# Tree attention on Trainium2: one quad of heads stored by two engines, by heads and by uneven partitions

## The chip, the cores and the metric

The kernel runs on one core of one Trainium2 chip. The metric is device microseconds of one launch. The core has five engines with instruction streams of their own: PE (TensorE, matrix products and transposes), DVE (VectorE), ACT (ScalarE), POOL (GpSimd) and SP (SyncE, which here only issues DMAs). Data moves between HBM and the on-chip memory through 16 DMA engines. GpSimd, SyncE and ScalarE issue transfers; each has its own queue (q0, q1 and q10 in the profile) on every one of the 16.

## The reference

Attention with 8 batches of 12 heads, 512 positions of 64 numbers, in float32. Position i may look only at itself and its ancestors in the binary tree in which the parent of i is (i - 1) // 2.

```python
for i in range(seq):
    mask[i, i] = 1
    parent = i
    while parent > 0:
        parent = (parent - 1) // 2
        mask[i, parent] = 1
scores = np.einsum('bhqd,bhkd->bhqk', Q, K) * scale + (1 - mask) * (-1e9)
weights = np.exp(scores - np.max(scores, axis=-1, keepdims=True))
weights = weights / (np.sum(weights, axis=-1, keepdims=True) + 1e-10)
return np.einsum('bhqk,bhkd->bhqd', weights, V).astype(np.float32)
```

The output is 96 heads x 512 x 64 float32, 12.58 MB; the first store is issued at 61.9 us.

## The kernel before, in words

The 96 heads are worked in 48 **pairs** (NP = 48, index i) and stored in 24 **quads** of four heads (NQ = 24, index q); quad q is done when the second of pairs 2q and 2q + 1 is. Position 4p + t of a head lies on partition p in slot t, so in HBM a partition's part of one head is one contiguous run of 4 x 64 float32, 1 KB.

For each pair, TensorE transposes K and Q (lines 401 and 433 in the steady part), adds mask codes to the scores by matrix products (458 and 491) and adds the products of K and Q (466 and 501). ScalarE takes the exponentials (476 and 507), TensorE multiplies by V with a column of ones (`values`, 551), and `norm` on VectorE divides by the sum (581, 582) into the output tile `of` of the quad, 128 partitions x 4 heads x 256. There are NOUT = 22 such tiles. The steady iteration is "SVK" or "SVQ": scores of pair i, values and norm of pair i - 1, transposes ahead.

All loads of K, Q and V but the first are issued by GpSimd, in an order written out in `pool_program` (lines 608 to 639); `pool(i)` emits as many of them after iteration i as `ready` allows. That list also has GpSimd's copies of V and the stores: `store` (589) writes one quad, 128 partitions x 4 heads x 1 KB = 512 KB. Eight of the stores stand among the loads, 13 at the list's end. The order in the list is the order of GpSimd's queue.

Quad 19, which holds pairs 38 and 39, is left out of that list. `store_apart` (600) gives it to SyncE after iteration 41, in two DMAs of all four heads: partitions 0 to 59 (240 KB) and 60 to 127 (272 KB). Quads 20 and 21 are GpSimd's again, its last two stores. The last two quads are stored by pairs (lines 768 and 769): SyncE issues two heads (256 KB) for each of pairs 44, 45 and 46 after iterations 45, 46 and 47. The last pair's heads go out singly: SyncE writes one (771), ScalarE the other (772), 128 KB each.

GpSimd's DMAs use eight completion semaphores in turn, so each of its DMAs waits until the eighth one before it has landed. SyncE's transfers share one queue per DMA engine and are worked there in the order of issue.

Of the kernel before, what the change touches and what calls it, by code (L numbers as in the profile page):

```python
# [119 lines left out]
def kernel(  # L120
# [7 lines left out]
    nc = tc.nc  # L128
    B, H, S, D = Q.shape
    P = nc.NUM_PARTITIONS  # L130
# [3 lines left out]
    NQ = NH // 4  # L134
# [17 lines left out]
    Or = out.rearrange("b h (p t) d -> p (b h) (t d)", t=4)  # L152
# [76 lines left out]
    qTs, kTs, kqs, obs, ets, ofs = {}, {}, {}, {}, {}, {}  # L229
# [365 lines left out]
        )  # L595


    APART, APART_AT, APART_ROWS = 19, 41, 60

    def store_apart():  # L600

        for p0, p1 in ((0, APART_ROWS), (APART_ROWS, P)):
            nc.sync.dma_start(
                out=Or[p0:p1, 4 * APART:4 * APART + 4, :],
                in_=ofs[APART][p0:p1, :, :, :].rearrange("p h t d -> p h (t d)"),
            )

    def pool_program():

        ops = [  # L610
            (load_k, 2, 2), (load_q, 2, 2), (load_v, 0, 4), (load_v, 4, 4),
            (load_k, 4, 2), (load_k, 6, 2), (load_q, 4, 2), (load_k, 8, 4),
            (load_q, 6, 2), (load_q, 8, 4), (load_v, 8, 8), (load_k, 12, 4),
            (load_q, 12, 4), (load_k, 16, 4), (load_rows, 1, "upper"),
            (load_q, 16, 4), (load_rows, 1, "even"), (load_k, 20, 4), (load_rows, 1, "odd"),
            (load_q, 20, 4), (load_k, 24, 8), (load_q, 24, 4), (load_rows, 2, "upper"),
            (load_q, 28, 4), (load_k, 32, 4), (load_rows, 2, "even", "odd"),
            (load_q, 32, 8), (load_k, 36, 4), (load_rows, 3, "upper"),
            (load_k, 40, 8), (load_rows, 3, "even", "odd"),
            (load_q, 40, 8), (spread_top, 2, 0, 16), (spread_top, 3, 0, 4), (load_q, 48, 4),  # L620
            (spread_top, 3, 4, 8), (load_k, 48, 8), (load_q, 52, 4), (spread_top, 3, 8, 12),
            (load_rows, 4, "upper"), (spread_top, 3, 12, 16),
        ]
        loaded, stored = 72, 0
        for h in range(56, NH, KB):
            top = [(spread_top, h // VB + 0)] if h % VB == 8 and 4 <= h // VB + 0 < NH // VB else []
            ops += [(load_k, h, KB)] + top + [(load_q, h, KB)]
            while loaded < min(h + 32, NH):
                names = ("even", "odd") if loaded % VB else ("upper",)
                ops.append((load_rows, loaded // VB) + names)  # L630
                loaded += KB
            if top:
                o = h // VB
                ops.append((spread_pool, (o, "X", 0, 16), (o, "Z1", 8, 16)))
            while 4 * stored + 4 + BEHIND <= h + KB:
                ops.append((store, nc.gpsimd, stored))
                stored += 1
        ops += [(store, nc.gpsimd, q) for q in range(stored, NQ - 2) if q != APART]
        return ops

    def ready(op, i):
# [62 lines left out]
    def spread_by(copy, table, steady, i):  # L704
# [5 lines left out]
        for args in todo:  # L710
            spread(copy, *args)

    program = pool_program()

    def pool(i):
# [21 lines left out]
    for i in range(NP + 1):  # L737
        steps = FIRST[i] if i < len(FIRST) else "SVK" if i % 2 else "SVQ"
        for step in steps:
# [11 lines left out]
            if step == "W":  # L751
                nc.scalar.copy(
                    out=codes[64:64 + CODE_ROWS, 1280:1536], in_=codes[0:CODE_ROWS, 1280:1536]
# [12 lines left out]
        if i == APART_AT:  # L766
            store_apart()
# [35 lines left out]
```

## Time and profile before

| what | value |
|---|---|
| median of 3 runs | 135.13 us (134.98 to 135.68) |
| the profiled execution's own time | 136.0 us |
| its span, first to last instruction | 132.8 us |
| around the span (136.0 - 132.8) | 3.2 us |
| busy: PE, DVE, ACT, POOL | 86%, 77%, 77%, 53% of the span |
| bytes read and written in HBM | 37.94 MB, 12.58 MB |
| mean granted TensorE clock | 0.979 |

A busy share is an average over the span. The page's second part shows each engine in 40 slices, a digit for tenths of busy time; for DMA it is the mean of the 16 DMA engines, so 8 may mean that all pause a little or that three have nothing to do. For every DMA the trace has a line with the time from issue to landing. It also holds the record of each packet (start, duration, size, queue) and of every update of a DMA's semaphore: each DMA engine that carries a part adds its share when that part has landed. All times in this document are us from the start of the span.

### The profile page before, as it was taken

Reading aid. Unit: us, or ns where it says so; the run is one execution under the profiler, and the core shown is the slowest. Engines: PE = TensorE matmul, PEld = TensorE weight load, DVE = VectorE, ACT = ScalarE, POOL = GpSimd, SP = SyncE. Lnnn points to the kernel's source line nnn. Section 1 sums busy time; section 2 is a strip of 40 time slices with the busy share of each in tenths; the row PEclk is TensorE's granted clock in tenths of the full one; section 3 lists DMA queues with packets and bytes.
Section 4 is the critical chain, followed back from the end, with each engine's and each line's share of the span. In section 5 each row is a group of like instructions: output and inputs, shape, how many; then the busy total and the mean of one; then the engine's idle time right before and its main releaser. Section 6 shows DMA issues by size and latency. Waiting matters only on the chain.

```text
span 132.8 us, 5554 instructions
## 1 busy us (share of the span) xinstructions
PE 114.1 (86%) x2414; PEld 79.2 (60%) x2417; DVE 101.8 (77%) x253; ACT 102.7 (77%) x169; POOL 70.6 (53%) x110
## 2 busy tenths in 40 slices
PE   6787969999899899779999999979898997989830
PEld 2344745766675677456775677657576675756520
DVE  3449769889999999945899998858796976757260
ACT  4379578988899999937899989958886987696900
POOL 6999525364343908999323369863976524512000
PEclk9999999999999999986999999999999999999996
DMA  3999999999999999999999999999999999999982
GB/s 98 245 189 192 199 198 200 201 202 206 200 202 203 202 204 198 209 205 201 205 204 196 316 254 204 292 274 242 330 214 335 233 297 402 401 399 397 373 322 70
DMA packets 32380, 32.25 MB, mean 243 GB/s; under 512 B 1341, under 2 KB 29629, under 8 KB 32357
## 3 DMA queue, kind: packets, MB, share of 16 engines
q0 software_dynamic: 29984, 29.63, 114.3%
q1 hardware_dynamic: 1813, 1.83, 4.0%
q10 hardware_dynamic: 560, 0.46, 1.1%
q8 instruction: 18, 0.29, 0.8%
q14 instruction: 5, 0.04, 0.1%
HBM read 37.94 MB, written 12.58 MB: 381 GB/s over the span
## 4 chain that ended last, share of the span: by engine, by line
DMA 38%; PE 29%; POOL 14%; issue 7%; ACT 5%; DVE 3%; POOLq 0%; ACTq 0%; DVEq 0%
DMA vst<-in_V_dram 20%; PE ob L551 10%; DMA qst<-in_Q_dram 10%; DMA kst<-in_K_dram 9%; PE s L458 4%; POOL vt L336 4%; PE s L491 3%; PE s L501 3%; PE qtp L433 3%; PE ktp L401 3%; PE s L466 3%; POOL kst L239 3%; POOL qst L239 3%; ACT e L507 3%; POOL vst L239 2%
## 5 line engine op out<-in xcount | busy, mean ns | idle before, releaser
L476 ACT ACTIVATE e<-s 128x1024 bf16<-128x1024 f32 x40 | 40.8, 1021 | 14.6 <-PE s L466 14.1
L551 PE MATMUL ob<-vt,e 128*128 128x65 bf16 (+1 forms) x940 | 37.9, 198 | 4.2 <-issue 2.0
L551 PEld LDWEIGHTS <-e 128*128 128x128 bf16 (+1 forms) x960 | 30.7, 103 | 12.5 <-issue 2.5
L507 ACT ACTIVATE e<-s 128x384 bf16<-128x384 f32 x80 | 34.6, 488 | 0.0
L582 DVE TENSOR_TENSOR of<-ob,rec 128x512 f32<-128x512 f32 x47 | 32.5, 691 | 1.6
L590 POOL DMA_DIRECT2D out_dram<-of x21 | 15.9, 761 | 16.7 <-DVE of L582 5.0
L336 DVE COPY vt<-vst 32x1024 bf16<-32x1024 bf16 (+6 forms) x46 | 19.7, 427 | 2.6 <-DMA vst<-in_V_dram 1.8
L581 DVE RECIPROCAL rec<-ob 128x8 f32<-128x8 f32 x47 | 9.7, 205 | 15.0 <-PE ob L551 14.7
L458 PE MATMUL s<-codes 40*128 40x512 bf16 x96 | 19.6, 398 | 0.8 <-ACT e L472 0.4
L466 PE MATMUL s<-kq 64*128 64x512 bf16 x96 | 18.8, 382 | 0.0
L336 POOL COPY vt<-vst 32x128 int32<-32x128 int32 (+2 forms) x32 | 15.7, 492 | 5.7 <-DMA vst<-in_V_dram 3.4
L280 POOL DMA_DIRECT2D vst<-in_V_dram x15 | 10.9, 728 | 10.6 <-DMA vst<-in_V_dram 5.4
L336 ACT COPY vt<-vst 32x512 int32<-32x512 int32 (+3 forms) x29 | 15.9, 550 | 0.7 <-DMA vst<-in_V_dram 0.2
L501 PEld LDWEIGHTS <-kq 64*128 64x128 bf16 x320 | 12.5, 95 | 5.4 <-issue 1.2
L501 PE MATMUL s<-kq 64*128 64x160 bf16 (+1 forms) x320 | 15.2, 211 | 0.5 <-issue 0.5
L441 DVE COPY kq<-qtp 128x1024 bf16<-128x1024 bf16 x20 | 13.6, 681 | 1.7 <-PE qtp L433 1.7
L491 PE MATMUL s<-codes 40*128 40x384 bf16 x80 | 13.9, 339 | 0.8
L433 PE MATMUL qtp<-ptile,qst 128*64 128x128 bf16 x320 | 12.5, 219 | 2.3 <-DMA qst<-in_Q_dram 1.7
L251 POOL DMA_DIRECT2D kst<-in_K_dram x12 | 9.0, 753 | 10.0 <-DMA kst<-in_K_dram 3.4
L401 PE MATMUL ktp<-ptile,kst 128*64 128x128 bf16 x320 | 13.0, 224 | 1.2 <-issue 0.8
L251 POOL DMA_DIRECT2D qst<-in_Q_dram x13 | 9.5, 733 | 6.9 <-PE qtp L433 2.1
L491 PEld LDWEIGHTS <-codes 40*128 40x128 bf16 x80 | 6.3, 95 | 10.8 <-issue 4.2
(42 smaller groups left out, 121.6 us busy)
## 6 DMA issues: line engine op xcount, KB each, us to landing
out_dram<-of POOLq DMA_DIRECT2D x21, 512.0 KB, 12.7
kst<-in_K_dram POOLq DMA_DIRECT2D x8, 512.0 KB, 13.5
qst<-in_Q_dram POOLq DMA_DIRECT2D x7, 512.0 KB, 13.9
vst<-in_V_dram POOLq DMA_DIRECT2D x12, 256.0 KB, 13.0
vst<-in_V_dram POOLq DMA_DIRECT2D x6, 512.0 KB, 13.0
qst<-in_Q_dram POOLq DMA_DIRECT2D x8, 256.0 KB, 11.0
kst<-in_K_dram POOLq DMA_DIRECT2D x6, 256.0 KB, 12.0
out_dram<-of SPq DMA_DIRECT2D x3, 256.0 KB, 5.4
```

The lines of the kernel that those rows point to most:

```text
L251: return nc.gpsimd.dma_start(out=kept[b][:, h0 % KB:h0 % KB + n, :, :].rearrange("p (g x) t d -> p g (x t d)", x=2), in_=wide[:, h0 // 2:( ...
L336: return copy(out=dst, in_=src)
L401: nc.tensor.transpose(out=columns(kp[64 * a:64 * a + 64, :], mixed, (256, 2), (leaves - mixed, 2), (1, 32)), in_=st[:, 2 * i % KB // 2 + a ...
L433: nc.tensor.transpose(out=halves[64 * a:64 * a + 64, :, c:c + 64], in_=st[:, 2 * i % KB // 2 + a, 4 * u + t, :], identity=ptile[:, 0:128],)
L458: nc.tensor.matmul(out=sp[:, a, :], lhsT=(k1code if i < WIDE else k1wide)[64 * a:64 * a + CODE_ROWS, :], rhs=(q1code[64 * a:64 * a + CODE_ ...
L466: nc.tensor.matmul(out=sp[:, a, :], lhsT=keys(i, a, TOP), rhs=qTs[i][64 * a:64 * a + 64, :, :].rearrange("p t c -> p (t c)"), start=False, ...
L476: ) if i < WIDE else nc.scalar.activation(
L491: nc.tensor.matmul(out=flat[:, a, :, :].rearrange("p u (t c) -> p u t c", t=4)[:, :, :, 16:64], lhsT=k2wide[64 * a:64 * a + CODE_ROWS, :], ...
L501: nc.tensor.matmul(out=flat[:, a, :, lo:hi], lhsT=keys(i, a, WTILE2[t]), rhs=qT[64 * a:64 * a + 64, :, lo:hi], start=False, stop=t == 1, s ...
L507: nc.scalar.activation(out=e2s[i % NE][:, a, :, 32:128].rearrange("p t (r u) -> p t r u", u=2), in_=flat[:, a, :, :].rearrange("p u (t r) ...
L551: nc.tensor.matmul(out=ob[lo:hi, a, 65 * t:65 * t + 65], lhsT=e[:, a, PLACE[t], lo:hi], rhs=vt[vtile[tile_v][0]][:, head(i, a) % VB, vtile ...
L582: nc.vector.tensor_tensor(out=ofs[q][:, head(i, a) % 4:head(i, a + n - 1) % 4 + 1:head(i, 1) - head(i, 0), :, :], in0=o4[:, a:a + n, :, 0: ...
```

## The change

Quad 19 is split by heads. SyncE stores heads 0 and 1 of it, as before in 60 and 68 partitions, after iteration 41. GpSimd stores heads 2 and 3 in 12 and 116 partitions, between quads 18 and 20 in its list. No bytes are added or taken away. `ready` treats the new entry as it does a store of quad 19.

```diff
-    APART, APART_AT, APART_ROWS = 19, 41, 60
+    APART, APART_AT, APART_ROWS, FEW_ROWS = 19, 41, 60, 12
+
+    def store_rows(eng, q, h0, *bounds):
+
+        for p0, p1 in zip(bounds, bounds[1:]):
+            eng.dma_start(
+                out=Or[p0:p1, 4 * q + h0:4 * q + h0 + 2, :],
+                in_=ofs[q][p0:p1, h0:h0 + 2, :, :].rearrange("p h t d -> p h (t d)"),
+            )
 
     def store_apart():
 
-        for p0, p1 in ((0, APART_ROWS), (APART_ROWS, P)):
-            nc.sync.dma_start(
-                out=Or[p0:p1, 4 * APART:4 * APART + 4, :],
-                in_=ofs[APART][p0:p1, :, :, :].rearrange("p h t d -> p h (t d)"),
-            )
+        store_rows(nc.sync, APART, 0, 0, APART_ROWS, P)
...
-        ops += [(store, nc.gpsimd, q) for q in range(stored, NQ - 2) if q != APART]
+        for q in range(stored, NQ - 2):
+            if q == APART:
+                ops.append((store_rows, nc.gpsimd, q, 2, 0, FEW_ROWS, P))
+            else:
+                ops.append((store, nc.gpsimd, q))
         return ops
```

## Prediction

> **What bounds the kernel now.** I read the slices first, then the stretches of the end, the chain of waits, the issue times of the stores, and last the single landings.
>
> In the page's slices the transfer engines stand at 9 from the second slice to the last but two:
>
> ```profile
> DMA  3999999999999999999999999999999999999982
> ```
>
> The table by stretches of the end (PE, PEld, DVE, ACT and POOL busy, clock, DMA share, GB/s) shows who is full there:
>
> ```profile
> 118.00:122.00 4.00, 3.28 (x78) 2.41 (x75) 2.40 (x7) 2.89 (x6) 0.75 (x1) 1.00 1.04 405
> 122.00:126.00 4.00, 3.42 (x66) 2.13 (x62) 1.53 (x3) 3.82 (x8) 0.00 (x0) 1.00 0.98 376
> 126.00:130.00 4.00, 1.17 (x22) 0.86 (x22) 2.02 (x6) 0.21 (x1) 0.00 (x0) 1.00 0.88 316
> 130.00:132.80 2.80, 0.00 (x0) 0.00 (x0) 0.00 (x0) 0.00 (x0) 0.00 (x0) 0.61 0.09 31
> ```
>
> The DMA share is about 1 until 126 us and 0.88 to 130: some of the 16 DMA engines have run out of work, others have not. The end of the chain of waits and the last stores on ACT's and SyncE's timelines:
>
> ```profile
> 127.46 0.42 DVE of L582
> 127.89 0.10 DVE rec L581
> 127.99 0.02 issue
> 128.01 0.43 DVE of L582
> ```
>
> ```profile
> 128.47 0.36 ACTq L590 DMA_DIRECT2D out_dram<-of  x1
> ```
>
> ```profile
> 110.32 0.93 SPq L603 DMA_DIRECT2D out_dram<-of  x2
> 122.66 5.61 SPq L590 DMA_DIRECT2D out_dram<-of  x4
> ```
>
> Compute ends at 128.44, the last store is issued at 128.47, and the span ends at 132.8. So two things bound the end: the compute chain, which the change does not touch, and how long the last store takes. From the DMA part:
>
> ```profile
> out_dram<-of SPq DMA_DIRECT2D x1, 272.0 KB
> ...
> out_dram<-of SPq DMA_DIRECT2D x1, 240.0 KB, 8.5
> ...
> out_dram<-of ACTq DMA_DIRECT2D x1, 128.0 KB, 3.1
> ```
>
> The 3.1 us of the last store is the number to take apart. The trace records a semaphore update for each DMA engine's share. ACT's store landed on ten engines between 130.03 and 130.18, on the other six at 130.48, 130.67, 130.88, 130.97, 131.26 and 131.56. Without a backlog it would be over at 130.18; the backlog of six engines costs 131.56 - 130.18 = **1.38 us**, all that a better balance can win.
>
> Who are the six? The 240 KB store (60 partitions) has 15 such landings, the 272 KB one (68 partitions) only **four**: 126.52, 126.70, 128.59, 128.89. It puts 17 rows, 68 packets of 1 KB, on each of four engines. Behind it SyncE's queue holds 16 + 16 + 16 + 8 packets per engine, and ACT's 8: 64 in all. Packets of 1 KB follow each other in 42.3 ns (packet records after 130 us), so 64 take 2.71 us; 128.59 and 128.89 plus 2.7 are 131.3 and 131.6, the two last landings. Two of the four engines with the 68 rows thus end the kernel; the other two are in time. The remaining four late engines carry only ordinary work; the worst lands at 130.97.
>
> How early are the others? SyncE's store of pair 44 (issued at 122.66) landed on three engines by 125.59, on seven between 127.37 and 128.09, on the six late ones from 128.48 to 129.55. A late engine's landing plus 2.01 is its last landing, so lateness begins at about 130.1 - 2.0 = 128.1: three engines have over 2 us of slack, seven have 0 to 0.7.
>
> **The change, part by part.** Bytes are the same (512 KB); only their placing changes.
>
> 1. *SyncE's two stores halve.* Fifteen engines have 4 rows of 2 KB where they had 4 of 4 KB: 8 packets fewer, 8 x 42.3 ns = -0.34 us. Four engines have 17 rows of 2 KB: 34 packets fewer, -1.44 us. Together -1.78 us on those four: 131.56 becomes 129.78, in time. These packets wait in a queue that takes turns with GpSimd's, so the saving is whole only because an engine is saturated until its end, which the late ones are. SyncE issues two DMAs as before, and nothing more until 122.66.
>
> 2. *GpSimd stores 12 rows.* Next to nothing: a row of 2 KB for each of twelve engines, half a 4 KB packet (GpSimd's 8 packets follow at 1.29 us, 161 ns each), +0.08 us.
>
> 3. *GpSimd stores 116 rows, 232 KB.* The trace has no such store. GpSimd's transfers have 128, 64 or 32 partitions, all on 16 engines. Bounds: over 16 engines at most 8 rows, 16 KB, +0.64 us; over four 29 rows, 58 KB, +2.34 us. SyncE's rows say which: 60 partitions went to 15 engines, 68 to 4, the mask's 40 to 10, each time the largest divisor up to 16. For 116 that is 4. I take four engines, though the rows are SyncE's.
>
> The Trainium skill, page "DMA: Bandwidth & Descriptors", section "Why a DMA increments its semaphore by 16 and not by 1", has this rule of divisors; SyncE's 15, 4 and 10 agree. For GpSimd it adds that the engines come from a turning cursor: the 12 rows would take engines 0 to 11 and the 116 rows 12 to 15, apart from SyncE's 0 to 3. No run here shows that yet.
>
> 4. *Where the four are.* A taken engine gains 2.34 - 0.34 = +2.0 us. With three early engines, the fourth has 0 to 0.7 us of slack, 0.35 in the middle: 130.1 + 2.0 - 0.35 = 131.75 against 131.56, **+0.2 us** (bounds -0.1 and +0.5). The four ordinary late ones get 0.26 earlier (130.71), so they no longer decide. I choose this because the engine that the 60 rows leave out is an early one, and four that are not SyncE's four are likeliest its neighbours.
>
> 5. *GpSimd's queue.* Two more issues, one store more (12 and 116 in, none out). Each issue takes 0.75 us:
>
> ```profile
> 113.07 0.75 POOL L590 DMA_DIRECT2D out_dram<-of  x1 [0.79 <-DMA out_dram<-of]
> 114.37 0.75 POOL L590 DMA_DIRECT2D out_dram<-of  x1 [0.54 <-DVE kq L420]
> 115.83 0.75 POOL L590 DMA_DIRECT2D out_dram<-of  x1 [0.71 <-DVE of L582]
> 120.83 0.75 POOL L590 DMA_DIRECT2D out_dram<-of  x1 [4.25 <-DVE of L582]
> ```
>
> Each store also waits until the eighth before it has landed everywhere (issue 113.07 after a landing at 112.53, 114.37 after 113.82, 115.83 after 115.28). The next such landings are 116.96, 119.29 and 120.55. So the 12 rows go at about 115.8, the 116 rows at 117.0 to 117.7, quad 20 at 119.3 instead of 115.83, quad 21 at about 120.8 as now, since its data comes then. Only these two stores wait behind. I cost quad 20's 3.5 us at nothing: the earlier stores keep the engines busy, the first engine ends quad 18 at 121.50, and that one has over 2 us of slack. If that cover were gone, engines without slack would stand idle up to about 1 us.
>
> Sum: the two 68-row engines leave the end (-1.4 us to the floor of 130.18), a 116-row engine takes their place at 131.75: +0.2 us. It is made in the profiled execution (span 132.8, own time 136.0); the 3.2 us around the span don't change, and so I move the median of 135.13 to **135.3 us**.
>
> **The rivals.**
>
> *The 116 rows spread over 16 engines.* Then 68-row engines get -1.78 + 0.72 (131.56 to 130.50), the worst ordinary late one -0.34 + 0.64 + 0.08 = +0.38: 131.35, 0.2 us less, 134.9 us. For it: all GpSimd transfers of the trace use 16 engines. Against: all of those have a multiple of 16. The same section of the Trainium skill reports as an exception that GpSimd gave some copies all 16 engines with rounded-up shares, 100 partitions on 15 of them; here that would be 8 rows on 14 engines and 4 on one. No run here shows it yet.
>
> *All four engines early (faster).* Then the end is the worst ordinary late engine, 130.97 - 0.26 = 130.71: -0.85 us, 134.3. For it: in another execution than the profiled one the seven may lie earlier. Against: only three engines have 2 us here.
>
> *A late engine among the four (slower).* The four ordinary late engines end between 130.48 and 130.97; +2.0 us makes 132.5 to 133.0, +0.9 to +1.4 us, 136.0 to 136.5. It turns the sign where a taken engine has less than 0.55 us of slack (130.1 + 2.0 - 131.56), and passes 0.5% where the engine is itself 0.15 us late. SyncE's own four are such a case, 131.56 - 1.78 + 2.34 = 132.1. For it: ten of 16 engines have under 0.5 us or none. Against: nothing in the profile, only the choice in step 4.
>
> *The order of issues does not act as written.* The instruction order shows the two new stores ahead of quads 20 and 21 on GpSimd and SyncE's halved ones in place, so this I leave out.
>
> **How the numbers follow.** A measurement of this kernel can tell about 0.5%, 0.68 us, from no change. Forecast 0.36 (of it 0.30 within 0.5%, 0.06 slower, as its bound is +0.5 us and profile and median differ); spread over 16: 0.19 (0.15 within, 0.04 faster); all early 0.18, faster; a late engine 0.27, slower. So faster 0.22, same 0.45, slower 0.33. The forecast's own range is 135.0 to 135.7. Both signs hold much of the chance, so the range reaches from the early case, 134.3, to the late one, 136.5.
>
> **What will show it.** The 116-row store's landings: four late ones beside updates at once would prove four engines; sixteen spread ones the first rival. The 68-row store should land by about 127 instead of 128.89. ACT's last store: its slowest engine at 131.4 to 132.1 and again alone at the end; at 130.7 with several together, the early case; at 132.5 or more, the late one. Quad 20's issue should move to about 119.3, quad 21's stay near 120.8, and compute end at 128.4. The prediction is wrong if compute moves, if engines idle before 126 us, or if the engines' order differs from execution to execution.

## The result, and the profile after

| | before | changed |
|---|---|---|
| median | 135.1 us (21 runs, 134.33 to 136.46) | 136.41 us (21 runs, 134.92 to 137.98) |
| ratio to before | | **1.0064**, 95% interval 1.0037 to 1.0091 |
| profiled execution: own time, span | 136.0, 132.8 us | 137.2, 134.1 us |

The ratio is 0.9 us on 135.1 (0.5 to 1.2); the medians of all runs lie 1.3 us apart. The ratios in this document leave out the runs over 1.5% longer than the fastest of their kernel, among them the profiled executions of the changed kernel, e2 and e8. The span of the changed kernel's profiled execution, 134.1 us, is in the middle of its 21 (133.1 to 135.4). Compute ended in it at another time than in the execution of before, so its landings are read against each other, not against those of before. The time lies in the range; but the forecast's case was +0.2 us, and this is the rival of a late engine, at the lower end of its price.

The slices of the changed kernel's page show DMA full nearly to the end again:

```profile
DMA  3999999999999999999999999999999999999970
```

The end of its chain of waits, ACT's last store, SyncE's stores, and the last rows of the table by stretches (columns as before):

```profile
127.39 0.02 issue
127.41 0.42 DVE of L582
```

```profile
127.87 0.35 ACTq L590 DMA_DIRECT2D out_dram<-of  x1
```

```profile
109.34 0.80 SPq L603 DMA_DIRECT2D out_dram<-of  x2
122.05 5.75 SPq L590 DMA_DIRECT2D out_dram<-of  x4
```

```profile
122.00:126.00 4.00, 3.52 (x74) 2.44 (x71) 1.20 (x5) 3.43 (x6) 0.00 (x0) 1.00 1.03 372
126.00:130.00 4.00, 0.60 (x14) 0.39 (x12) 1.75 (x5) 0.00 (x0) 0.00 (x0) 0.78 0.89 326
130.00:134.10 4.10, 0.00 (x0) 0.00 (x0) 0.00 (x0) 0.00 (x0) 0.00 (x0) 0.50 0.11 37
```

Compute ended at 127.83, in this execution 0.6 us earlier than in that of before; the span is 1.3 us longer all the same. So the time went behind compute. The DMA part (KB each, us from issue to landing):

```profile
out_dram<-of POOLq DMA_DIRECT2D x1, 232.0 KB, 9.3
out_dram<-of SPq DMA_DIRECT2D x1, 136.0 KB
out_dram<-of SPq DMA_DIRECT2D x1, 128.0 KB, 5.5
out_dram<-of ACTq DMA_DIRECT2D x1, 128.0 KB, 4.8
...
out_dram<-of POOLq DMA_DIRECT2D x1, 24.0 KB, 9.1
```

The last two stores, issued after everything else, take 5.5 and 4.8 us where they took 3.3 and 3.1. ACT's store landed on the 16 engines at these times:

```
before  130.03 130.05 130.06 130.07 130.09 130.10 130.10 130.11 130.15 130.18 130.48 130.67 130.88 130.97 131.26 131.56
changed 129.42 129.45 129.47 129.48 129.49 129.66 129.79 130.00 130.10 130.14 130.16 131.07 131.14 131.61 131.81 132.64
```

Before, the last is 1.5 us behind the first, and the lateness is shared by six. Now it is 3.2 us, and one engine stands alone at the end.

Which engines are these? The packet records of GpSimd's 116-row store tell. They name no engine, but on each engine a packet starts where the one before it ends, so that its packets can be followed. (A packet's end here comes some 0.4 us before the landing that the semaphore records.) Its 232 KB are 4 x 14 packets of 4,096 B and 4 of 2,048 B, thus 29 rows on each of **four** engines; the other twelve have 14 records of 16 B and one of 8 B in their place. The 12-row store left 12 packets of 2,048 B and, on four engines, a lone record of 8 B. These four had ended quad 18 at 121.61, 123.60, 123.79 and 124.67: places 2, 7, 9 and 14 of the 16. From the second on, the 116 rows end at 125.95, 126.14 and 127.31, quad 20 lands on these at 127.99, 128.18 and 129.57, and ACT's last store at 131.61, 131.81 and 132.64: the three last. Only the earliest of the four had the room.

GpSimd's queue is the other thing that moved:

```profile
114.99 0.75 POOL L590 DMA_DIRECT2D out_dram<-of  x1 [0.58 <-DVE of L582]
116.66 0.60 POOL L603 DMA_DIRECT2D out_dram<-of  x1 [0.92 <-DVE rec L581]
118.47 1.29 POOL L603 DMA_DIRECT2D out_dram<-of  x1 [1.21 <-DMA out_dram<-of]
119.76 0.78 POOL L590 DMA_DIRECT2D out_dram<-of  x1
120.97 0.77 POOL L590 DMA_DIRECT2D out_dram<-of  x1 [0.42 <-DVE kq L441]
```

Quad 20 is issued at 119.76 instead of 115.83, quad 21 at 120.97. This is the rival theory for the experiments: that the two extra DMAs, with at most eight in flight, delay the last quads.

### The profile page after: what moved, and what is told of

Same layout as the page of the kernel before. It is cut to its first block, busy times and chain, and to the rows that moved or that the text cites. A ratio compares the mean times of both kernels' runs of the same rounds, so it can differ in the third digit from the quotient of the medians.

```text
span 134.1 us, 5557 instructions
## 1 busy us (share of the span) xinstructions
PE 113.5 (85%) x2414; PEld 78.6 (59%) x2417; DVE 100.8 (75%) x253; ACT 102.3 (76%) x169; POOL 72.5 (54%) x112
## 4 chain that ended last, share of the span: by engine, by line
DMA 30%; PE 30%; DVE 16%; ACT 7%; POOL 7%; issue 5%; ACTq 0%; POOLq 0%
DMA vst<-in_V_dram 13%; PE ob L551 10%; DMA qst<-in_Q_dram 10%; DMA kst<-in_K_dram 7%; DVE of L582 6%; PE s L458 4%; DVE vt L336 4%; ACT e L476 3%; POOL vt L336 3%; PE s L466 3%; PE ktp L401 3%; PE qtp L433 3%; PE s L491 3%; PE s L501 2%; ACT e L507 2%
## 5 line engine op out<-in xcount | busy, mean ns | idle before, releaser
L336 DVE COPY vt<-vst 32x1024 bf16<-32x1024 bf16 (+6 forms) x46 | 18.8, 409 | 3.8 <-DMA vst<-in_V_dram 2.2
```

What stands on the lines that cost most here:

```text
L336: return copy(out=dst, in_=src)
```

## The experiments

**Theory:** the 116 rows add 2 us to four engines, and the time depends on how late these are. **Rival:** GpSimd's queue. Ratios are to the kernel before, on the same chip, from 9 to 17 runs of each changed kernel (six of e6, three of e8). Compute ends between 127.5 and 130.7 us in the profiled executions of these kernels, so landings are compared within one list, the 16 landings of one store. A straggler is an engine that lands well behind all others of its list.

| kernel | GpSimd's part of quad 19 | most on one engine | ratio (95%) |
|---|---|---|---|
| changed | 12, 116 | 58 KB on four | 1.0064 (1.0037 to 1.0091) |
| e1 | 128 | 16 KB | 0.9990 (0.9951 to 1.0030) |
| e5 | 16, 112 | 16 KB | 1.0010 (0.9980 to 1.0040) |
| e9 | 12, 116, head by head | about 18 KB | 1.0003 (0.9978 to 1.0027) |
| e4 | 116, 12 | 58 KB on four (by the cursor, SyncE's) | 1.0028 (0.9990 to 1.0065) |
| e2 | 4, 116, 8 | 58 KB on four | 1.0034 (0.9995 to 1.0072) |
| e3 | 8, 116, 4 | 58 KB on four | 1.0071 (1.0030 to 1.0111) |
| e6 | quads 18 and 19: 12, 116 | 116 KB on four | 1.0219 (1.0175 to 1.0263) |
| e8 | 45, 83 | 166 KB on one | 1.0316 (1.0270 to 1.0362) |
| e7 | one head: 45, 83 | 9 KB | 0.9993 (0.9958 to 1.0028) |

### e1: GpSimd's half in one DMA

```diff
-                ops.append((store_rows, nc.gpsimd, q, 2, 0, FEW_ROWS, P))
+                ops.append((store_rows, nc.gpsimd, q, 2, 0, P))
```

> The changed kernel, but GpSimd stores heads 2 and 3 of quad 19 in one DMA of 128 partitions, so over all 16 engines (16 KB each). Theory (the place of the 116 rows sets the end): an engine that already ends late gains only 0.64 - 0.34 = 0.3 us and SyncE's 68-row engines lose 1.78 - 0.64 = 1.1, so the last landing is near that of before, -0.2 to +0.2 us: ratio to before 0.998 to 1.002, and the landings of the last store have no single straggler. Rival (GpSimd's queue: one more DMA among eight in flight delays quads 20 and 21): some of the changed kernel's +0.6% stays, ratio 1.003 to 1.006, with quad 20 issued at about 117.0 instead of 115.8 us.

0.9990. The division of the quad between two queues, with GpSimd's part spread evenly, neither gains nor loses measurably. ACT's store lands last on three engines together, at 131.45, 131.47 and 131.55, 0.67 us behind the next (130.78): no single straggler. The interval's end, 1.0030, touches the rival's 1.003, so this run alone doesn't decide.

### e5: the same DMAs, in even pieces

```diff
-                ops.append((store_rows, nc.gpsimd, q, 2, 0, FEW_ROWS, P))
+                ops.append((store_rows, nc.gpsimd, q, 2, 0, 16, P))
```

> The changed kernel, but GpSimd stores its two heads in 16 and 112 partitions in place of 12 and 116. The number of GpSimd's DMAs, its issues and its waits are those of the changed kernel, but both pieces go over all 16 engines (2 and 14 KB each). Theory (the place of the 116 rows): as with the single DMA of 128 partitions, ratio to before 0.996 to 1.002, no straggler among the last landings. Rival (GpSimd's queue with its eight DMAs in flight): the changed kernel's 1.004 to 1.009.

1.0010. Number, order and waits of GpSimd's DMAs are the change's, and its timeline shows the same delay, quad 20 at 120.26:

```profile
115.97 0.53 POOL L603 DMA_DIRECT2D out_dram<-of  x1 [0.58 <-DVE rec L581]
117.25 0.68 POOL L603 DMA_DIRECT2D out_dram<-of  x1 [0.75 <-DMA out_dram<-of]
120.26 0.77 POOL L590 DMA_DIRECT2D out_dram<-of  x1 [2.33 <-DVE kq L420]
121.63 0.76 POOL L590 DMA_DIRECT2D out_dram<-of  x1 [0.61 <-DVE of L582]
```

The cost is gone all the same. So it isn't the queue: the earlier stores cover quad 20's delay, as the prediction held.

### e4, e2, e3: the same rows on other engines

```diff
-                ops.append((store_rows, nc.gpsimd, q, 2, 0, FEW_ROWS, P))
+                ops.append((store_rows, nc.gpsimd, q, 2, 0, 116, P))      # e4
+                ops.append((store_rows, nc.gpsimd, q, 2, 0, 4, 120, P))   # e2
+                ops.append((store_rows, nc.gpsimd, q, 2, 0, 8, 124, P))   # e3
```

What was expected, in the order e4, e2, e3:

> The changed kernel, but GpSimd stores 116 rows first and then 12: by the cursor the 116 rows fall on engines 0 to 3, which carry SyncE's 68 rows too. Theory: the slower two of these four engines go from 131.56 by -1.78 + 2.34 to 132.1, +0.5 us: ratio 1.003 to 1.005, and the last landings are those of the same engines as the 68-row store's late ones. Rival (GpSimd's queue): the same DMAs as the changed kernel in another order, so its 1.006.

> The changed kernel, but GpSimd stores 4 rows, then 116, then 8: if a cursor deals out the engines, the 116 rows fall on engines 4 to 7. Theory: the time changes with the group alone. Of engines 4 to 11 two are early, one is in the middle and five are late by the packet records of the changed kernel; if 4 to 7 hold the early ones, only one late engine is loaded, and the end is set by that one: ratio 1.003 to 1.008; if they hold four late ones, 1.008 to 1.012. The 116-row store's landings come in four classes that show which. Rival (GpSimd's queue): one DMA more than the changed kernel, so 1.006 to 1.010 whichever the group, the same as for the 8-row and the 0-row forms.

> The changed kernel, but GpSimd stores 8 rows, then 116, then 4: by the cursor the 116 rows fall on engines 8 to 11. Theory: if these are all late engines, each gains 2.0 us and the latest of them sets the end at 132.5 to 133.0 in the time of the profiled execution of before: ratio 1.007 to 1.011, at least as slow as engines 12 to 15; if they hold early ones, 1.003 to 1.008. Rival (GpSimd's queue): the same time as with 4 rows first, within 0.3%.

1.0028, 1.0034 and 1.0071. In each the records show four engines with 14 packets of 4,096 B and one of 2,048 B. What differs is who they are. In the change the engine that SyncE's 60 rows leave out has the 116 rows; in e4, e2 and e3 it has the small records, and in e2 the 8 rows and in e3 the last 4. That is what the Trainium skill says of GpSimd ("DMA: Bandwidth & Descriptors", section "Why a DMA increments its semaphore by 16 and not by 1"): the engines of a store are dealt out by a turning cursor.

The last landings follow. e2 has one straggler, 133.64 behind 132.16; e3 has two, 133.87 and 133.40 behind 132.41; in e4 the last engine, at 132.36, is one of the four that had the 116 rows (they end there at 126.60), the next is at 131.57. The order e4, e2, e3 is as expected, but the intervals of the three overlap one another and that of the change: that the groups differ in price is supported, not shown. Compute, too, ended at 130.4 and 130.7 in the profiled executions of e2 and e3, 2 us later than in that of before, so not all of these two lengths is the stragglers'. The intervals of e4 and e2 also reach down to no cost at all; of the kernels with 116 rows on four engines, the change, e3 and e6 are clear of it.

### e6: the cost twice

```diff
+            elif q == 18:
+                ops.append((store, nc.gpsimd, q, 0, 2))
+                ops.append((store_rows, nc.gpsimd, q, 2, 0, FEW_ROWS, P))
```

> The suspected cost twice: quad 18 too is split, heads 0 and 1 in one DMA of 128 partitions, heads 2 and 3 in 12 and 116, all by GpSimd. Engines 12 to 15 get 58 - 16 = 42 KB more, at 40 ns a KB 1.7 us. Theory: the end moves by nearly all of it, since three of these four engines had no slack left: 1.006 + 0.012, ratio 1.013 to 1.020, and in the last store's landings three stragglers 3 us behind the rest. Rival (GpSimd's queue): two DMAs more, as the change added two: ratio 1.010 to 1.014, landings without such stragglers but quads 20 and 21 issued later.

1.0219, more than either expected. ACT's store lands from 130.85 on, on the last four engines at 133.44, 134.28, 134.52 and 135.04. The theory's stragglers are there, four where it had three, and the table by stretches of e6 shows the DMA engines mostly idle behind them (share 0.40 and 0.05):

```profile
130.00:134.00 4.00, 0.00 (x0) 0.00 (x0) 0.00 (x0) 0.00 (x0) 0.00 (x0) 0.50 0.40 142
134.00:136.40 2.40, 0.00 (x0) 0.00 (x0) 0.00 (x0) 0.00 (x0) 0.00 (x0) 0.50 0.05 19
```

The step from the change is 0.0155 x 135.1 = 2.1 us for 1.7 us of work. The two intervals allow 1.7; if the 0.4 is real, its cause stays open.

### e7: a version meant to be faster

```diff
-        store_rows(nc.sync, APART, 0, 0, APART_ROWS, P)
+        store_rows(nc.sync, APART, 0, 3, 0, APART_ROWS, P)
...
-                ops.append((store_rows, nc.gpsimd, q, 2, 0, FEW_ROWS, P))
+                ops.append((store_rows, nc.gpsimd, q, 3, 1, 0, 45, P))
```

Here and in e9 `store_rows` takes the number of heads as an argument.

> A version that the theory suggests: SyncE stores three heads of quad 19 in 60 and 68 partitions, GpSimd the fourth in 45 partitions (15 engines, 3 KB each, which leaves the cursor at 15) and 83, a prime, so one engine: 83 KB on engine 15, which ended quad 21 over 3 us before the latest. Theory: SyncE's four engines end 0.7 us earlier than before (66 KB against 84), the late ordinary ones as before (15 against 16 KB), engine 15 in time: -0.4 to -0.7 us, ratio 0.995 to 0.998. Rival (GpSimd's queue): two DMAs more than before, 1.003 to 1.009. If the cursor was not at 15, the 83 KB fall on another engine and end the kernel 2 to 3 us later, 1.012 to 1.022.

0.9993: no gain. Its premise failed. The 83 rows of a single head did not go to one engine: the records are 13 times 4,096 + 2,048 B (6 rows), one engine with 5 rows, and 16 and 8 B on two. Engine 15 stayed empty, and the late ones got 5 KB more than before. The last landings are fourteen engines from 130.20 to 130.69 and two at 131.52 and 131.54. What these two have in common: in the trace, quads land on one engine 1.2 us or more behind all others from 118.63 on (the next is at 117.18), after an instruction packet of 16 KB that took 1.03 us from 116.55; a second falls back after the packet at 123.67. Before has the like (119.29 beside 118.37, after the packet at 116.60). It goes with those packets in time; that they are the cause was not tried.

### e8: the 83 rows with two heads

```diff
-                ops.append((store_rows, nc.gpsimd, q, 2, 0, FEW_ROWS, P))
+                ops.append((store_rows, nc.gpsimd, q, 2, 0, 45, P))
```

> The changed kernel, but GpSimd stores its two heads in 45 and 83 partitions. In the version with three heads on SyncE the 83 partitions of a single head did not go to one engine: the records show 13 engines with 6 rows, one with 5, two with none. Here the store has two heads, as the 116 rows of the change had, which went to four engines. Theory (divisor rule for a store of two heads, place sets the end): 83 is a prime, all 166 KB fall on one engine, by the cursor engine 15, which was over 3 us early: 166 KB at 40 ns a KB are 6.7 us, so it ends 3 to 4 us after the others, ratio 1.020 to 1.030, one straggler in the last landings. Rival (the 83 rows spread as the single head's did): 12 KB each, no straggler, ratio 0.997 to 1.003.

1.0316. With two heads the rule of divisors holds: one engine has 41 packets of 4,096 B and one of 2,048 B, the other fifteen 41 records of 16 B each. ACT's store lands on it at 134.80 and SyncE's last at 136.85, 3.3 us after the next (133.51). One engine out of 16 sets the time of the kernel. GpSimd takes 2.56 us to issue this DMA, and from 122 to 126 us the engines move 229 GB/s, where those of the change moved 372:

```profile
118.75 2.56 POOL L603 DMA_DIRECT2D out_dram<-of  x1 [1.65 <-DMA out_dram<-of]
```

```profile
122.00:126.00 4.00, 3.51 (x72) 2.43 (x71) 1.23 (x4) 3.54 (x6) 0.85 (x2) 1.00 0.95 229
126.00:130.00 4.00, 0.71 (x16) 0.50 (x14) 1.82 (x6) 0.00 (x0) 0.00 (x0) 0.77 1.04 350
130.00:134.00 4.00, 0.00 (x0) 0.00 (x0) 0.00 (x0) 0.00 (x0) 0.00 (x0) 0.50 0.39 141
134.00:138.00 4.00, 0.00 (x0) 0.00 (x0) 0.00 (x0) 0.00 (x0) 0.00 (x0) 0.50 0.04 15
```

From 122 to 126 us 13 of the 203 packets of 4,096 B took from 0.3 to 2.3 us, where the usual one takes 0.165 (in the change 7 of 342, none over 0.5). The late issue is a likely reason for that, and for a time above the expected 1.020 to 1.030, not a tested one.

### e9: the change's rows, head by head

```diff
-                ops.append((store_rows, nc.gpsimd, q, 2, 0, FEW_ROWS, P))
+                for h in (2, 3):
+                    ops.append((store_rows, nc.gpsimd, q, h, 1, 0, FEW_ROWS, P))
```

> The change's own rows, 12 and 116, but head by head: four GpSimd DMAs of one head each in place of two of two heads. Bytes and rows as in the change. Theory (a store of a single head spreads over up to 16 engines in rounded-up shares, and the place sets the end): the 116 rows go 8 to an engine on 14 engines, 4 on one, so there is no straggler and the time is that of the even forms, ratio 0.997 to 1.004, though there are two DMAs more than in the change. Rival 1 (116 rows always take four engines; for each head the same four, as 12 + 116 turn the cursor once round): the change's 1.004 to 1.009. Rival 2 (GpSimd's queue): two DMAs more than the change, 1.006 to 1.012, without a straggler.

1.0003. The same rows of the same heads, in two DMAs more, with quads 20 and 21 issued later than in any other kernel here, and the cost is gone:

```profile
122.43 0.78 POOL L590 DMA_DIRECT2D out_dram<-of  x1 [1.01 <-DVE of L582]
123.72 0.77 POOL L590 DMA_DIRECT2D out_dram<-of  x1 [0.52 <-DVE rec L581]
```

Its DMA part has the four stores as

```profile
out_dram<-of POOLq DMA_DIRECT2D x2, 116.0 KB, 7.2
...
out_dram<-of POOLq DMA_DIRECT2D x2, 12.0 KB, 8.3
```

and the records have no run of 14 packets or of 14 small records: the 116 rows of one head are spread. ACT's last landings are 130.70, 131.17, 131.37, 131.73 and 132.30, where e8 has one 1.8 us behind the next. Together with e5 this settles it: neither the bytes, nor the rows, nor the number of DMAs, nor the delay of quad 20 costs the time. That the rows go to four engines does. With the four engines two side effects went too, the small records on the other twelve and the longer issue. Neither can be the cost: 14 records at 7 ns are 0.1 us, on engines that are not among the last three, and all that a longer issue can delay, quads 20 and 21, came later in e5 and e9.

## Why the prediction was right and wrong

*What bounds the end:* right. The last stores' slowest DMA engine set the end in every trace here.

*Step 1, SyncE's halves:* right in effect. The 68 rows landed at 121.23, 121.32, 121.34 and 121.37, and their four engines are not the last three. The landing was foretold for about 127; that it came over 5 us earlier enters no term of the sum.

*Steps 2 and 3, twelve engines, then four:* right. The 116 rows took 2.35, 2.35 and 2.64 us on the three that ended last, from the end of quad 18 to that of the last packet, against 2.34.

*Step 4, where the four are:* **this failed.** "With three early engines, the fourth has 0 to 0.7 us of slack" gave 131.75 for the last landing. Only one of the four was early. The reason given, that they are likeliest neighbours of the engine that the 60 rows leave out, was right about the place (by the cursor) and wrong about what it means: the three early engines do not stand together. e2 and e3 say the same of the groups beside, each with stragglers. Three engines without 2 us of slack, not one, then got 2 us: two from the middle of the order (places 7 and 9) and a late one (place 14), and these three end the last store at 131.61, 131.81 and 132.64. The rival had priced the worst late one at 130.97 + 2.0 = 133.0, and the changed kernel's list ends at 132.64 with compute 0.6 us earlier.

*Step 5, GpSimd's queue:* right in cost, e5 and e9 show none. Quad 20 was foretold for 119.3 and came at 119.76, quad 21 for 120.8 and came at 120.97. The issue of the 116 rows was taken for 0.75 us at 117.0; it took 1.29 at 118.47, since the eighth DMA before it landed last at 118.19.

*The sum:* the two 68-row engines left the end, as said; what took their place was +0.9 us (0.5 to 1.2) instead of +0.2. That the time still lies in the range is no merit of step 4: the range reached from one rival to the other.

*The rivals:* the spread over 16, priced at -0.2 us, was built by e1, e5 and e9: -0.1, +0.1 and 0.0 us, each with 0.3 to 0.5 us to either side. The late engine, +0.9 to +1.4, had a chance of 0.27 and came true. It had "nothing in the profile" against it, and for it ten engines of 16 with under 0.5 us. Outside SyncE's four there were twelve, four of them late: blind draws of four miss all the late ones in 70 of 495 cases. The draw is not quite blind, as the four stand together; but the weight was given to a guess about neighbours instead of to that count.

*The signs of being wrong:* the engines were busy until 126 (DMA share 1.03 from 122 to 126). Compute ended at 127.83, not 128.4; whether the change moves it, or the order of the engines differs between executions, one trace per kernel can't tell. The 21 spans of the changed kernel are a hint at such differences: eight of them are at most 133.8, near the 133.0 to 133.2 that are the kernel before's medians in the rounds of e1, e5 and e8, and thirteen are 134.1 to 135.4. So 0.9 us is a mean over executions that differ.

## What to carry to other kernels

A store whose partition count is no multiple of 16 can land on a few DMA engines, and a kernel that ends in a drain of stores ends with its slowest engine. So read the landings of the last store engine by engine before moving bytes, and put extra rows only on engines that the trace shows to be early; one trace shows one execution. What a split does is told by the packet records, not by the row count.

## What the runs showed of the hardware

- GpSimd's stores of two heads followed the divisors (12 partitions on 12 engines, 116 on 4, 83 on 1); those of a single head did not: 83 partitions went 6 rows to each of 13 engines and 5 to another, and 116 were spread too. The Trainium skill's page "DMA: Bandwidth & Descriptors" (the section named above) has both, the second as an exception for some copies; these runs tie it to the store having one head, that is one run of 1 KB per partition.
- An engine that has no part in such a store still gets records: 14 of 16 B beside four engines' 29 rows, 41 beside one engine's 83. The issue grows with it: 0.75 us for a whole quad, 1.29 for 116 rows on four engines, 2.56 for 83 on one.
- The 16 engines are not equally far: in the profiled execution of before, quad 18 ended on them over a stretch of 4.2 us (121.50 to 125.73).
